# Row sums on one core: the last store as two 64-partition transfers, from SyncE and ScalarE

## The chip, the cores and the metric

The kernel runs on one core of a Trainium2 chip. The metric is the device time of one execution in microseconds (us); less is better. The engines that matter are VectorE (DVE), ScalarE (ACT) and SyncE (SP), which issues DMA transfers. A transfer works on 16 DMA engines and adds 16 in total to a semaphore as its parts land.

## The reference

The input is 67.11 MB of float32, and each row of 1,024 numbers is summed to one number:

```python
batch, seq, dim = 32, 512, 1024
x = np.random.randn(batch, seq, dim).astype(np.float32)

def reference(x):
    return np.sum(x, axis=-1).astype(np.float32)
```

## The kernel before

There are 16,384 rows, 128 for each partition. They are taken as two blocks: in the first, partition p holds 113 neighbouring rows, in the second 15 (`BLOCKS`). Rows are loaded in groups of up to 16 per partition into three buffers in turn (`xt`, `BUFS`), so that a load of group b waits until the buffer of group b - 3 has been read. DVE sums a whole group with one TENSOR_REDUCE (`rows_dve`); ACT sums some rows of the late groups one by one (`rows_act`).

Nothing is scheduled by a planner: each engine runs its instructions in the order in which `row_sums` writes them, and waits on semaphores that are set by hand. All loads are issued by SP (line 139), in the order of the list `loads`. The first two of them are moved ahead of the program's opening barrier.

The order is made so that little is left once the last bytes have come. One row per partition is loaded first (`lead`). The last 16 rows of block 0 (columns `z0` to `Z` of `res_z`) come last: three pieces cut at `CUTS`, and then the very last row in two parts (`tail`), 576 and 448 numbers wide, each summed by a DVE instruction of its own (`pairs_dve`, line 75). The second part takes the sum of the first as its first element.

The sums go out in three stores, all from SP. Two early stores (line 145) carry all columns that are done before the last 16; they are issued once `piece2` has landed. The last store (lines 146 to 148) carries the last 16 columns of block 0: 128 partitions with 64 bytes each. It waits for DVE's last count (`vec`) and for ACT's last count (`act`). Each instruction of ACT or DVE that ends a sum adds 1 to its engine's semaphore.

Behind the last store SP waits for the early stores (line 151), clears the semaphores below `store` (line 152), and then waits until `store` is 16 and takes the 16 off again (line 153). That wait is the last instruction of the program.

Of the kernel before, what the change touches and what calls it, by code (L numbers as in the profile page):

```python
# [13 lines left out]
CUT = 576  # L14
CUTS = (0, 9, 13, 15)
EARLY = 2


def row_sums(nc, x: bass.AP, out: bass.AP):
    P = nc.NUM_PARTITIONS  # L20
# [6 lines left out]
    xs, outs = [], []  # L27
# [14 lines left out]
    x_z, res_z = xs[0], sums[0]  # L42
    Z = BLOCKS[0]
    z0 = Z - G
# [3 lines left out]
    sems = {n: nc.alloc_semaphore(n) for n in names}  # L48
    slots = [sems[f"slot{i}"] for i in range(BUFS)]
    vec, act = sems["vec"], sems["act"]  # L50
# [3 lines left out]
    count = {"vec": 0, "act": 0}  # L54
# [88 lines left out]
    for k, n in enumerate(BLOCKS):  # L143
        end = z0 if k == 0 else n
        nc.sync.dma_start(out=outs[k][:, 0:end], in_=sums[k][:, 0:end]).then_inc(sems["early_store"], 16)
    nc.sync.wait_ge(vec, count["vec"])
    nc.sync.wait_ge(act, count["act"])
    nc.sync.dma_start(out=outs[0][:, z0:Z], in_=res_z[:, z0:Z]).then_inc(sems["store"], 16)


    nc.sync.wait_ge(sems["early_store"], 16 * len(BLOCKS))
    nc.sync.sem_clear(range(numbers[0], sems["store"].num))
    nc.sync.wait_ge(sems["store"], 16).then_inc(sems["store"], -16)


def kernel(tc: tile.TileContext, x: bass.AP, out: bass.AP):
    tc.close()
    tc.compile()  # L158
    nc = tc.nc
    row_sums(nc, x, out)  # L160

    sp = mybir.EngineType.SP
    fn = nc.m.functions[0]
    entry, body = None, None
    for blk in fn.blocks:
        ops = [i for i in blk.instructions if i.engine == sp]
        if entry is None:
            entry = blk  # L170
        elif any(i.opcode == "DMACopy" for i in ops):
            body = blk
            break
    code = list(body.instructions)
    loads = [i for i in code if i.engine == sp and i.opcode == "DMACopy"][:EARLY]
    for load in loads:
        assert not load.sync_info.on_wait
        code.remove(load)
    body.instructions = code
    code = list(entry.instructions)  # L180
    at = next(k for k, i in enumerate(code) if i.engine == sp and i.opcode == "Drain")
    code[at:at] = loads
    entry.instructions = code
# [29 lines left out]
```

## Time and profile before

| | us |
|---|---|
| median of 3 runs | 160.58 (160.57 to 160.62) |
| the profiled execution | 160.63 |
| its span, first to last instruction | 159.3 |
| DVE busy in the span | 121.6 (76%) |
| ACT busy in the span | 17.2 (11%) |
| HBM read | 67.11 MB, 422 GB/s over the span |
| last store, issue to landing | 1.4 (8.0 KB) |

The profile shows one execution. Its times count from the first instruction in the span. A line such as L75 is a line of the kernel; SPq stands for SP's DMA issues, whose duration is the time that SP needs to hand a transfer over and not the time in which data moves. The DMA share of a stretch is the mean busy share of the core's 16 DMA engines. Waiting is not counted as busy.

### The profile page before, as it was taken

Reading aid. Unit: us, or ns where it says so; the run is one execution under the profiler, and the core shown is the slowest. Engines: PE = TensorE matmul, PEld = TensorE weight load, DVE = VectorE, ACT = ScalarE, POOL = GpSimd, SP = SyncE. Lnnn points to the kernel's source line nnn. Section 1 sums busy time; section 2 is a strip of 40 time slices with the busy share of each in tenths; the row PEclk is TensorE's granted clock in tenths of the full one; section 3 lists DMA queues with packets and bytes.
Section 4 is the critical chain, followed back from the end, with each engine's and each line's share of the span. In section 5 each row is a group of like instructions: output and inputs, shape, how many; then the busy total and the mean of one; then the engine's idle time right before and its main releaser. Section 6 shows DMA issues by size and latency. Waiting matters only on the chain.

```text
span 159.3 us, 108 instructions
## 1 busy us (share of the span) xinstructions
DVE 121.6 (76%) x17; ACT 17.2 (11%) x31; POOL 0.2 (0%) x4
## 2 busy tenths in 40 slices
DVE  1100029999499995999869996899959999797685
ACT  3000000000000000000000000000000000394694
POOL 0000000000000000000000000000000000000000
DMA  9969979989699699699699797996996999699994
GB/s 395 527 263 527 477 313 527 411 378 527 280 510 527 263 527 527 263 527 510 280 527 444 346 527 313 477 527 263 527 510 278 463 494 494 296 444 444 395 400 143
DMA packets 2304, 67.18 MB, mean 422 GB/s; under 512 B 640, under 2 KB 768, under 8 KB 1024
## 3 DMA queue, kind: packets, MB, share of 16 engines
q1 hardware_dynamic: 2304, 67.18, 98.1%
HBM read 67.11 MB, written 0.07 MB: 422 GB/s over the span
## 4 chain that ended last, share of the span: by engine, by line
DMA 75%; DVE 22%; SPq 1%; issue 0%
DMA xt<-in_x_dram 51%; DMA tail<-in_x_dram 24%; DVE res L57 22%; SPq L139 1%; DVE pairs L75 0%; DVE res L75 0%
## 5 line engine op out<-in xcount | busy, mean ns | idle before, releaser
L57 DVE TENSOR_REDUCE res<-xt 128x16 f32<-128x16384 f32 (+3 forms) x9 | 118.7, 13191 | 32.5 <-DMA xt<-in_x_dram 32.5
L68 ACT ACTIVATE xt<-xt 128x1024 f32<-128x1024 f32 x15 | 15.6, 1043 | 138.1 <-DMA xt<-in_x_dram 138.1
L68 ACT ACTIVATION_READ_ACCUMULATOR xt<-xt 128x1 f32 x15 | 2.8, 187 | 0.0
L57 DVE TENSOR_REDUCE res<-lead 128x1 f32<-128x1024 f32 x1 | 1.2, 1220 | 1.4 <-DMA lead<-in_x_dram 1.4
L103 DVE MEMSET tail<- 128x1 f32 x1 | 0.1, 59 | 2.0 <-PEq L158 2.0
L68 ACT ACT_TABLE_LOAD x1 | 1.3, 1283 | 1.9 <-PEq L158 1.9
L75 DVE CUSTOM_DVE_ANT_0 pairs<-tail 128x288 f32<-128x288 f32 (+1 forms) x2 | 0.9, 426 | 0.1
L75 DVE CUSTOM_DVE_ANT_0 pairs<-xt 128x512 f32<-128x512 f32 x1 | 0.7, 692 | 0.2 <-DMA xt<-in_x_dram 0.2
L75 DVE DVE_READ_ACCUMULATOR2_ANT res<- 128x1 f32 x2 | 0.2, 82 | 0.0
L197 POOL MEMSET const-uint8-127<- 128x1 uint8 x1 | 0.1, 103 | 0.0
L197 POOL MEMSET const-bfloat16-1.0<- 128x1 bf16 x1 | 0.1, 102 | 0.0
L197 POOL MEMSET const-float32-0.0<- 128x1 f32 x1 | 0.1, 98 | 0.2 <-issue 0.2
L197 POOL MEMSET const-float32-1.0<- 128x1 f32 x1 | 0.1, 98 | 0.0
L75 DVE DVE_READ_ACCUMULATOR2_ANT tail<- 128x1 f32 x1 | 0.1, 80 | 0.0
## 6 DMA issues: line engine op xcount, KB each, us to landing
xt<-in_x_dram SPq DMA_DIRECT2D x1, 7680.0 KB, 39.6
xt<-in_x_dram SPq DMA_DIRECT2D x1, 4608.0 KB, 31.2
xt<-in_x_dram SPq DMA_DIRECT2D x1, 2048.0 KB, 35.7
xt<-in_x_dram SPq DMA_DIRECT2D x1, 1024.0 KB, 37.7
lead<-in_x_dram SPq DMA_DIRECT2D x1, 512.0 KB, 3.4
tail<-in_x_dram SPq DMA_DIRECT2D x1, 288.0 KB, 37.9
tail<-in_x_dram SPq DMA_DIRECT2D x1, 224.0 KB, 38.0
xt<-in_x_dram SPq DMA_DIRECT2D x6, 40.8
```

The lines of the kernel that those rows point to most:

```text
L57: nc.vector.tensor_reduce(out=res[:, c : c + n], in_=t[:, j * D : (j + n) * D].rearrange("p (j d) -> p j d", d=D), axis=X, op=ADD,).then_i ...
L68: nc.scalar.activation(out=v, in_=v, func=COPY, accum_out=res[:, c + i : c + i + 1]).then_inc(act, 1)
L75: nc.vector.tensor_tensor_reduce(out=pairs[:, 0 : h - a], in0=t[:, a:h], in1=t[:, h:b], scale=1.0, scalar=0.0, op0=ADD, op1=ADD, accum_out ...
L103: nc.vector.memset(tail[:, CUT + 15 : CUT + 16], 0.0).then_inc(vec, 1)
L139: nc.sync.dma_start(out=dst, in_=src).then_inc(s, 16)
L197: nc = _bacc.Bacc("TRN2", target_bir_lowering=False, num_devices=1)
```

## The change

The last store becomes two transfers. SP stores partitions 0 to 63, and ACT stores partitions 64 to 127; both add to `store`, which now has to reach 32. ACT waits for both counts before its transfer, and its wait for `vec` adds 1 to `act`. SP's two waits stand in the other order in the source. Ahead of clearing the semaphores SP now also waits for that extra count of `act`, so that ACT's waits are over by then.

```diff
+HALF = 64
...
+    nc.sync.wait_ge(act, count["act"])
     nc.sync.wait_ge(vec, count["vec"])
-    nc.sync.wait_ge(act, count["act"])
-    nc.sync.dma_start(out=outs[0][:, z0:Z], in_=res_z[:, z0:Z]).then_inc(sems["store"], 16)
-
-
+    nc.sync.dma_start(out=outs[0][0:HALF, z0:Z], in_=res_z[0:HALF, z0:Z]).then_inc(sems["store"], 16)
+    nc.scalar.wait_ge(act, count["act"])
+    nc.scalar.wait_ge(vec, count["vec"]).then_inc(act, 1)
+    nc.scalar.dma_start(out=outs[0][HALF:P, z0:Z], in_=res_z[HALF:P, z0:Z]).then_inc(sems["store"], 16)
+
+
+    nc.sync.wait_ge(act, count["act"] + 1)
     nc.sync.wait_ge(sems["early_store"], 16 * len(BLOCKS))
     nc.sync.sem_clear(range(numbers[0], sems["store"].num))
-    nc.sync.wait_ge(sems["store"], 16).then_inc(sems["store"], -16)
+    nc.sync.wait_ge(sems["store"], 32).then_inc(sems["store"], -32)
```

## The prediction

> **What bounds the kernel now.** I read the page first, then the chain of waits, then the waits of SyncE (SP), then the DMA activity of single stretches. The share line under the chain says that this is a load-bound kernel:
>
> ```profile
> DMA 75%; DVE 22%; SPq 1%; issue 0%
> ```
>
> The change does not touch that part. The chain in order of time (start, duration, what) shows where the loads stop deciding, and on the way it gives prices that I need for SP's DMA issues:
>
> ```profile
> 1.85 0.06 issue
> 1.92 40.18 DMA xt<-in_x_dram
> ...
> 117.56 0.33 SPq L139
> 117.89 0.04 issue
> 117.93 0.44 SPq L139
> 118.37 0.04 issue
> 118.42 0.46 SPq L139
> 118.88 0.04 issue
> 118.92 0.45 SPq L139
> ...
> 119.41 37.98 DMA tail<-in_x_dram
> 157.40 0.02 issue
> 157.42 0.40 DVE pairs L75
> 157.82 0.01 DVE res L75
> ```
>
> The last load lands at 157.40, DVE reduces it by 157.82, and all that is left is the last store. So the change can move only the 1.48 us from 157.82 to the end of the span at 159.30. SP's waits in this stretch (who waited, for whom, us in total, times, longest) are:
>
> ```profile
> SPq L153 <- SPq L153: 1.0, 1, 1.0
> SPq L148 <- DVE res L75: 0.5, 1, 0.5
> ...
> SPq L147 <- ACT xt L68: 0.3, 1, 0.3
> ```
>
> Source line 146 waits for `vec` and line 147 for `act`, but what ran is one wait instruction for `act` (L147), over early, and the wait for `vec` carried by the transfer itself (L148). So the transfer starts 0.03 us after DVE's end. The final wait (L153) then sits for 1.0 us. The rows by stretch say what happens inside that time; the last two columns are the DMA engines' busy share and GB/s:
>
> ```profile
> 157.82:158.18 0.36, 0.00 (x1) 0.00 (x0) 0.00 (x0) 1.00 0.00 0
> 158.18:158.68 0.50, 0.00 (x0) 0.00 (x0) 0.00 (x0) 1.00 0.00 0
> 158.68:158.90 0.22, 0.00 (x0) 0.00 (x0) 0.00 (x0) 1.00 0.36 38
> 158.90:159.30 0.40, 0.00 (x0) 0.00 (x0) 0.00 (x0) 1.00 0.00 0
> ```
>
> The store is 0.36 of hand-over and issue (the issue itself 0.33), 0.50 in which nothing moves, 0.22 of packets, and 0.40 until SP has seen the completion. The packets keep an engine busy for only 0.36 x 0.22 = 0.08 us. What a split halves, the rows, is at most the 0.22; the other 1.26 us is latency that each half pays again, though side by side if the two are independent.
>
> **The change part by part.** The profiled execution took 160.63 us, 1.33 more than its span; the median of the runs is 160.58. I take the 1.33 as it is, and add my differences to the median.
>
> *The order of the two waits.* Built, the changed program has on SP a wait instruction for `vec`, and then a transfer that carries the wait for `act`. The late semaphore is now on the separate instruction, so that instruction and the step to the next one lie on the path. On ScalarE (ACT) it is the same: one wait instruction for `vec` and `act` that also adds 1 to `act`, then the transfer. In the trace such a wait lasts 0.017 us, and from the end of the barrier's wait to SP's next DMA it is 0.06 (the chain's first piece). So both halves are issued at 157.82 + 0.03 + 0.02 + 0.06 = 157.93 instead of 157.85: **+0.08**. Low end +0.06, with the 0.04 that lies between SP's successive issues; high end +0.14, with the 0.12 that DVE took after the same barrier's wait.
>
> *SP's half.* Its queue has been in use all along. I take the old 0.33 + 0.50 + 0.22 + 0.40, so it ends 0.08 later than before.
>
> *ACT's half.* No row shows ACT issue a DMA. ACT's last instruction ends at 157.27, so it is idle for 0.55 us before `vec` arrives, and nothing is queued behind the transfer. The nearest row for a first use of a queue is SP's first transfer, `lead`, and its stretches:
>
> ```profile
> 0.00:0.38 0.38, 0.00 (x0) 0.00 (x0) 0.15 (x4) 1.00 0.00 0
> 0.38:1.00 0.62, 0.00 (x0) 0.00 (x0) 0.05 (x2) 1.00 0.00 0
> 1.00:1.20 0.20, 0.00 (x0) 0.00 (x0) 0.00 (x0) 1.00 1.48 246
> ```
>
> It took 0.38 to issue and another 0.62 to the first packet, against 0.33 and 0.50 for the last store: 0.05 + 0.12 = **+0.17**. That row is a load, and part of its 0.12 can belong to that; 0 is the low end. I take 0.17, since ACT's queue is as fresh as SP's was then. The high end is open; I treat more than this as a rival.
>
> *The packets.* Each half has 64 rows over the same 16 engines. If the 0.22 is proportional to the rows it becomes 0.11 (-0.11); if the engines' staggered starts make it up it stays; one completion record more on each engine adds 0.01. I take **0**: with 0.08 of work in 0.22 the stretch is mostly stagger, and that does not depend on the rows. [...]
>
> *The end.* `store` has to reach 32. The 16 increments came within 0.16 us before; the two sets could queue for up to that, but ACT's set comes 0.17 after SP's in this sum, so I take **0**.
>
> *What SP does besides.* The wait for `early_store`, the wait for ACT's extra `act` increment and the clearing come after the issue and before the final wait, some 0.1 us more than before. The 1.0 us of L153 hides them; without it they would cost that 0.1. The clearing cannot catch ACT still waiting, and ACT's increment is there by 157.9. No queue but ACT's own is passed: no load or compute changes place.
>
> Sum: 0.08 + 0.17 = **+0.25**, so 160.83 (0.16% more). Adding the ends gives -0.05 (0.06 - 0.11) to +0.48 (0.14 + 0.17 + 0.01 + 0.16), so 160.53 to 161.06 for this case alone. A difference of 0.2%, 0.32 us, is about what a measurement of this kernel can tell from no change: below 160.26 is faster, above 160.90 slower.
>
> **The rivals.**
>
> *B, slower: the two issues get in each other's way, and the change does not do what it says.* In the chain, an issue that follows at once on another takes 0.44 to 0.46 instead of 0.33, whatever its size, and the starts lie 0.37 (117.56 to 117.93), then 0.49 and 0.50 apart. Something is held for about 0.49 us by each transfer. If it belongs to SP's sequencer, ACT is free of it; if SP and ACT share it, ACT's half (or SP's) trails by 0.37 to 0.49. Then the sum is 0.08 + 0.43 = +0.51, 161.09; the ends are 0.08 + 0.37 - 0.11 = +0.34 (160.92), and 0.08 + 0.49 + 0.17 = +0.74 (161.32). It decides from a trailing of 0.24 on. Against it: this trace has one issuing engine only, so the row is equally well a matter of that engine. [...]
>
> *C, slower: ACT's first transfer costs far more than SP's first did*, in the issue or outside the span. The only thing that ACT fetches in this trace is its table, a row of 1.28 us. A start between the +0.32 that would be told and such a fetch gives 160.90 to 160.58 + 0.08 + 1.28 = 161.94. Nothing in the profile speaks for it but that ACT has never issued a DMA here; SP's cheap first use speaks against it.
>
> *D, faster: the latency shrinks with the rows.* All of SP's transfers have 128 rows, so this trace cannot say whether the 0.49 that something is held depends on the rows. If it does, 64 rows hold it for 0.24, the first packet comes 0.24 earlier and the stretch of packets loses up to 0.11: 0.08 - 0.24 = -0.16, to -0.27 (160.42 to 160.31). If the whole 0.83 before the first packet and half the 0.22 went, 0.08 - 0.42 - 0.11 = -0.45 (160.13). Against it: issues that followed at once cost 0.44 to 0.46 for 224 KB (the second of `tail`) as for 2,048 KB (117.93), so the bytes do not set the price; whether the rows do is open.
>
> **How the numbers follow.** The case summed above gets 0.40: of it 0.34 is within 0.2%, and 0.06, its upper end, beyond. B gets 0.27, all slower. C gets 0.12, all slower. D gets 0.13: 0.07 faster, 0.06 within. For what I have not thought of, 0.08: 0.02 faster, 0.03 within, 0.03 slower. Together faster 0.09, within 0.43, slower 0.48. The likeliest single case stays within 0.2%, so its 160.83 is the forecast, though most of the rest lies above it. The range 160.30 to 161.35 holds the case, all of B and the part of D that is not told from no change; outside are about 0.07 of D, 0.09 of C and 0.03 of the rest.
>
> **What would show it.** In the changed profile I look for: both transfers' issue at 0.11 after DVE's end (the order of the waits); ACT's issue at about 0.38 and SP's at 0.33 (0.44 or more on either, started together, is B); the first packets 0.50 after SP's issue and 0.62 after ACT's; the last packet to the end unchanged at 0.40. C would be a long issue or a silent stretch of over 0.8 on ACT's half, or more than 1.33 outside the span; D a first packet under 0.7 us after the issue's start. The forecast is wrong if the span's growth comes to less than 0 or more than 0.5.

## The result and the profile after

The changed kernel takes 161.26 us (median of 6 runs, 161.12 to 161.37) against 160.62 for the kernel before in the same runs: 0.64 us more, a ratio of 1.0036 with a 95% interval of 1.0026 to 1.0047. It is slower by more than 0.2%. The time lies in the predicted range; the forecast itself, 160.83, had 0.25 of the 0.64.

The chain of the changed kernel is made of the same parts as before, so the loss has to be sought behind it:

```profile
DMA 74%; DVE 22%; SPq 1%; issue 0%
```

In the timeline, the last lines are DVE's final read-out and the two issues of the split store (start, duration, engine, line):

```profile
157.81 0.08 DVE L76 DVE_READ_ACCUMULATOR2_ANT res<- 128x1 f32 x1
157.97 0.53 SPq L149 DMA_DIRECT2D out_dram<-res  x1
158.03 0.53 ACTq L152 DMA_DIRECT2D out_dram<-res  x1
```

The two transfers do start nearly together. But each issue takes 0.53 where the single one took 0.33, and both are equally long. SP's waits show that the late semaphore moved from the transfer to the wait instruction (L148, `vec`), and that the final wait (L158) grew from 1.0 to 1.3:

```profile
SPq L158 <- SPq L158: 1.3, 1, 1.3
...
SPq L148 <- DVE res L76: 0.9, 1, 0.9
```

By stretch, with the DMA engines' share and GB/s in the last two columns:

```profile
157.90:157.97 0.07, 0.00 (x0) 0.00 (x0) 0.00 (x0) 1.00 0.00 0
157.97:158.50 0.53, 0.00 (x0) 0.00 (x0) 0.00 (x0) 1.00 0.00 0
158.50:159.14 0.64, 0.00 (x0) 0.00 (x0) 0.00 (x0) 1.00 0.00 0
159.14:159.34 0.20, 0.00 (x0) 0.00 (x0) 0.00 (x0) 1.00 0.21 21
159.34:159.41 0.07, 0.00 (x0) 0.00 (x0) 0.00 (x0) 1.00 0.00 0
159.41:159.61 0.20, 0.00 (x0) 0.00 (x0) 0.00 (x0) 1.00 0.21 21
159.61:160.00 0.39, 0.00 (x0) 0.00 (x0) 0.00 (x0) 1.00 0.00 0
```

SP's half moves from 159.14 and ACT's half from 159.41. The engines rest between the two, so the halves do not overlap at all. Each half needs 0.20 for 64 rows, nearly as much as 128 rows needed (0.22), and the last stretch has not changed.

The table takes the trace's records apart from DVE's last end to the end of the span, in us. Start is the step to the issue, silent the time from the issue's end to the first packet, packets the time from the first packet's start to the last one's, rest the time from the last packet's start to the end. The experiments below are in it too. Where two halves end apart, the half that ends last is shown.

| kernel | half | start | issue | silent | packets | rest | sum |
|---|---|---|---|---|---|---|---|
| before | SP, 128 rows | 0.03 | 0.33 | 0.50 | 0.20 | 0.42 | 1.48 |
| changed | ACT, 64 | 0.14 | 0.53 | 0.85 | 0.19 | 0.40 | 2.10 |
| sp_half | SP, 64 | 0.03 | 0.53 | 0.64 | 0.19 | 0.39 | 1.77 |
| act_alone | ACT, 128 | 0.13 | 0.37 | 0.51 | 0.20 | 0.42 | 1.63 |
| split_warm | ACT, 64 | 0.14 | 0.53 | 0.85 | 0.18 | 0.42 | 2.12 |
| split_late | ACT, 64 | 1.20 | 0.52 | 0.66 | 0.18 | 0.40 | 2.96 |
| swap_only | SP, 128 | 0.08 | 0.33 | 0.50 | 0.21 | 0.42 | 1.53 |
| col_split | ACT, 128 | 0.13 | 0.37 | 0.51 | 0.19 | 0.50 | 1.70 |
| split_96_32 | ACT, 32 | 0.13 | 0.38 | 0.50 | 0.16 | 0.51 | 1.68 |
| split_96_32_carried | ACT, 32 | 0.03 | 0.40 | 0.51 | 0.16 | 0.53 | 1.63 |
| split_64_carried | ACT, 64 | 0.03 | 0.54 | 0.90 | 0.19 | 0.39 | 2.05 |

Between the first two rows lie 0.62 us: 0.11 in the start, 0.19 in the issue, 0.35 in silence, and about -0.02 each in the packets and the rest. The other 0.07 of the span's growth lies ahead of DVE's last end (157.90 against 157.82). That end differs by more among the profiled runs of this study, from 157.69 to 158.17, in kernels whose loads are the same, so I do not put it down to the change.

### The profile page after: what moved, and what is told of

The parts are those of the page before. It is cut to its first block, busy times and chain, and to the rows that moved or that the text cites. A ratio compares the mean times of both kernels' runs of the same rounds, so it can differ in the third digit from the quotient of the medians.

```text
span 160.0 us, 111 instructions
## 1 busy us (share of the span) xinstructions
DVE 121.6 (76%) x17; ACT 17.2 (11%) x31; POOL 0.2 (0%) x4
## 4 chain that ended last, share of the span: by engine, by line
DMA 74%; DVE 22%; SPq 1%; issue 0%
DMA xt<-in_x_dram 51%; DMA tail<-in_x_dram 24%; DVE res L58 22%; SPq L140 1%; DVE pairs L76 0%; DVE res L76 0%
```

## The experiments

My first reading of the two equal issues was rival B: two engines that issue at once slow each other. The first four runs set this against two others: that a transfer of 64 rows is dearer by itself, and that the first use of ACT's queue is. Kernels that ran together share their runs of the kernel before; its median was 160.88, 160.63 and 160.68 in the three groups of four. The times given are medians; the ratios are estimated from all runs of both kernels and can differ a little from the quotient of the medians.

### SP's half alone (sp_half)

```diff
-    nc.sync.dma_start(out=outs[0][:, z0:Z], in_=res_z[:, z0:Z]).then_inc(sems["store"], 16)
+    nc.sync.dma_start(out=outs[0][0:64, z0:Z], in_=res_z[0:64, z0:Z]).then_inc(sems["store"], 16)
```

> SP alone stores partitions 0 to 63 with the waits of before; ACT stores nothing, and the last 16 columns of partitions 64 to 127 are left out. In the changed kernel SP's half took 0.53 to issue and 0.65 more to its first packet, against 0.33 and 0.50 before. Contention (SP's and ACT's issues slow each other): alone, 64 rows take 0.33 and 0.50 again, 160.5 to 160.6. Shape (a transfer of 64 rows costs more to issue than one of 128): 0.53 and 0.65, some 160.96. Rows (fewer rows, shorter latency): under 0.33 and under 0.50, 160.4 or less.

Measured: 161.13 against 160.88, ratio 1.0016 (1.0007 to 1.0026). Half the work, with nothing on ACT, is slower than all of it. The issue in the timeline, and the silent stretch in the rows by stretch:

```profile
158.19 0.53 SPq L148 DMA_DIRECT2D out_dram<-res  x1
```

```profile
158.71:159.35 0.64, 0.00 (x0) 0.00 (x0) 0.00 (x0) 1.00 0.00 0
159.35:159.55 0.20, 0.00 (x0) 0.00 (x0) 0.00 (x0) 1.00 0.21 21
```

These are the changed kernel's figures for SP's half, without a second issuer. Contention does not make them, and neither does the latency fall from 128 rows to 64. What is left is the shape, which the sweeps further down take apart.

### ACT alone with the whole store (act_alone)

```diff
-    nc.sync.dma_start(out=outs[0][0:HALF, z0:Z], in_=res_z[0:HALF, z0:Z]).then_inc(sems["store"], 16)
...
-    nc.scalar.dma_start(out=outs[0][HALF:P, z0:Z], in_=res_z[HALF:P, z0:Z]).then_inc(sems["store"], 16)
+    nc.scalar.dma_start(out=outs[0][:, z0:Z], in_=res_z[:, z0:Z]).then_inc(sems["store"], 16)
...
```

> ACT alone makes the whole last store, 128 rows, as the first and only transfer of its queue; SP issues nothing then. In the changed kernel ACT's half took 0.53 to issue and 0.85 to its first packet. Contention: 0.33 to 0.38 and about 0.50, so only the later start on ACT is left, 160.7 to 160.8. A slow first use of ACT's queue: 0.53 and 0.85 stay, 161.2. Shape: as contention.

Measured: 161.05 against 160.88, ratio 1.0012 (1.0003 to 1.0022).

```profile
158.06 0.37 ACTq L151 DMA_DIRECT2D out_dram<-res  x1
```

```profile
158.43:158.94 0.51, 0.00 (x0) 0.00 (x0) 0.00 (x0) 1.00 0.00 0
158.94:159.15 0.21, 0.00 (x0) 0.00 (x0) 0.00 (x0) 1.00 0.38 39
```

ACT's first transfer costs 0.04 more to issue than SP's store and 0.01 more of silence. The 0.10 of the later start is most of its loss of 0.15 behind DVE's end. A slow first use is out.

### ACT's queue used before (split_warm)

```diff
...
+    nc.scalar.dma_start(out=warm[:, :], in_=xs[0][:, 0:16]).then_inc(sems["warm"], 16)
...
```

> The changed kernel with one small load (8 KB into a scratch tile that nothing reads) issued by ACT at the start, so that the store is not the first transfer of ACT's queue. Contention: the store's issues stay at 0.53 and ACT's half at 0.85 to the first packet, 161.2 to 161.3. Slow first use: ACT's half falls to SP's figures or to 0.33 and 0.50, 160.8 to 161.0.

Measured: 161.48 against 160.88, ratio 1.0036 (1.0023 to 1.0049), as the changed kernel; ACT's half at 0.53 and 0.85 as before. The use of the queue lay some 156 us ahead of the store, so a queue that cools within that time is not excluded by this run alone; act_alone, never used before and cheap, excludes it.

### ACT's half later (split_late)

```diff
-    nc.scalar.wait_ge(act, count["act"])
-    nc.scalar.wait_ge(vec, count["vec"]).then_inc(act, 1)
+    nc.scalar.wait_ge(vec, count["vec"])
+    nc.scalar.activation(out=lead[:, :], in_=lead[:, :], func=COPY).then_inc(act, 1)
+    nc.scalar.wait_ge(act, count["act"] + 1).then_inc(act, 1)
...
-    nc.sync.wait_ge(act, count["act"] + 1)
+    nc.sync.wait_ge(act, count["act"] + 2)
```

> The changed kernel with one ACTIVATE of 128x1024 (about 1.05 us, its result is not used) between ACT's wait and its transfer, so that SP's half has its first packets before ACT issues. Contention: both halves go back to 0.33 of issue and about 0.50 to the first packet; the end comes about 1.1 us later than with one store, 161.8 to 161.9. Shape: 0.53 and 0.65 for SP's half all the same, and the end at 162.2 or more. Slow first use: SP's half at 0.33 and 0.50, ACT's half at 0.53 and 0.85, 162.3.

Measured: 162.30 against 160.88, ratio 1.0089 (1.0074 to 1.0104). ACT's issue and its silence, when SP has long been done:

```profile
159.37 0.52 ACTq L153 DMA_DIRECT2D out_dram<-res  x1
```

```profile
159.89:160.54 0.65, 0.00 (x0) 0.00 (x0) 0.00 (x0) 1.00 0.00 0
```

The issue stays long without company. The silence falls from 0.85 to 0.66 by the records (the stretch above has 0.65, its ends being rounded). So there is contention too, in the silence of the half that comes second: 0.19 us. SP's half kept 0.52 and 0.64.

### Which shapes are dear (shapes)

```diff
+    nc.sync.wait_ge(sems["store"], 16)
+    nc.sync.dma_start(out=outs[0][0:128, z0:Z], in_=res_z[0:128, z0:Z]).then_inc(sems["probe"], 16)
+    nc.sync.wait_ge(sems["probe"], 16)
+    nc.sync.dma_start(out=outs[0][0:64, z0:Z], in_=res_z[0:64, z0:Z]).then_inc(sems["probe"], 16)
+    nc.sync.wait_ge(sems["probe"], 32)
...
```

> The kernel of before, and behind its last store thirteen small transfers by SP, each waiting for the one ahead to land, so that each is alone: stores of 128, 64 (0 to 63), 64 (64 to 127), 32, 96, 112, 120 and 16 partitions with 16 columns, 128 partitions with 8 columns, 64 with 32, loads of 128 and 64 partitions with 16 columns, and the first again. SP's half alone took 0.525 to issue and 0.64 to its first packet. Full width is the cheap case: 0.33 and 0.50 wherever all 128 partitions take part, 0.52 or more and over 0.6 in all others, also for 112. Count by engine (it follows the rows): a graded price, dearest at 16 rows and near 0.33 at 112. Bytes (4 KB is dearer than 8 KB): 64 partitions with 32 columns are as cheap as 128 with 16, and 128 with 8 as dear as 64 with 16. Place in the output alone: the loads do not differ.

In the timeline the stores of L153 to L165 have 128, 64, 64, 32, 96, 112 and 120 partitions, the two loads of L173 and L175 have 128 and 64:

```profile
159.43 0.33 SPq L153 DMA_DIRECT2D out_dram<-res  x1
160.87 0.54 SPq L155 DMA_DIRECT2D out_dram<-res  x1
162.62 0.47 SPq L157 DMA_DIRECT2D out_dram<-res  x1
164.30 0.35 SPq L159 DMA_DIRECT2D out_dram<-res  x1
165.68 0.33 SPq L161 DMA_DIRECT2D out_dram<-res  x1
167.09 0.32 SPq L163 DMA_DIRECT2D out_dram<-res  x1
168.49 0.38 SPq L165 DMA_DIRECT2D out_dram<-res  x1
...
174.33 0.36 SPq L173 DMA_DIRECT2D lead<-in_x_dram  x1
175.97 0.52 SPq L175 DMA_DIRECT2D lead<-in_x_dram  x1
```

Each line is one transfer of one execution. None of my four guesses holds. The dear ones are the four transfers of 64 partitions, stores and load, and only they. Their silence is 0.65 to 0.66 for stores (0.76 for the load, against 0.61 for the load of 128); the stores of all other counts have 0.43 to 0.50. Here are the silent stretches of the first 64 and of the 96:

```profile
161.41:162.05 0.64, 0.00 (x0) 0.00 (x0) 0.00 (x0) 1.00 0.00 0
166.00:166.50 0.50, 0.00 (x0) 0.00 (x0) 0.00 (x0) 1.00 0.00 0
```

The bytes do not matter here (64 partitions with 32 columns are as dear, 0.47 to issue, 128 with 8 as cheap, 0.36). Alone and from start to start, 64 partitions took 1.75 and 1.68 us, 128 took 1.44, 32 took 1.38 and 16 took 1.31.

### The same split by columns (col_split)

```diff
-    nc.sync.dma_start(out=outs[0][0:HALF, z0:Z], in_=res_z[0:HALF, z0:Z]).then_inc(sems["store"], 16)
+    nc.sync.dma_start(out=outs[0][:, z0:z0 + 8], in_=res_z[:, z0:z0 + 8]).then_inc(sems["store"], 16)
...
-    nc.scalar.dma_start(out=outs[0][HALF:P, z0:Z], in_=res_z[HALF:P, z0:Z]).then_inc(sems["store"], 16)
+    nc.scalar.dma_start(out=outs[0][:, z0 + 8:Z], in_=res_z[:, z0 + 8:Z]).then_inc(sems["store"], 16)
```

> The changed kernel with the halves cut by columns: SP stores the first 8 of the 16 last columns of all 128 partitions, ACT the other 8. Waits and engines as in the changed kernel. If the price is that of a transfer of 64 partitions: both issues at 0.33 to 0.37, SP's first packet 0.50 later, and the time between before and the changed kernel, +0.15 to +0.35 over before (the upper end if ACT's half still trails by the 0.19 of the two meeting). If the price is that of 4 KB transfers or of two engines issuing at once: 0.53 each and +0.6.

Measured: 160.86 against 160.63, ratio 1.0013 (1.0004 to 1.0022). Two engines issue at the same time as in the changed kernel, and the issues are short:

```profile
157.99 0.33 SPq L149 DMA_DIRECT2D out_dram<-res  x1
158.05 0.37 ACTq L152 DMA_DIRECT2D out_dram<-res  x1
```

ACT's silence is 0.51, the same as alone: with this shape the second half does not trail. What is left is the later start (0.10), ACT's longer issue (0.04) and a rest of 0.50 instead of 0.42.

### The order of the waits alone (swap_only)

```diff
-    nc.sync.wait_ge(vec, count["vec"])
-    nc.sync.wait_ge(act, count["act"])
+    nc.sync.wait_ge(act, count["act"])
+    nc.sync.wait_ge(vec, count["vec"])
```

> The kernel of before with SP's last two waits in the order of the changed kernel, and one transfer of 128 partitions as before. The wait for vec becomes an instruction of its own: SP's transfer starts 0.07 after DVE's end instead of 0.03, +0.05. If the order of the waits were a main part of the loss, +0.3 or more.

SP's waits show `vec` on its own instruction (L147), as in the changed kernel:

```profile
SPq L147 <- DVE res L75: 0.9, 1, 0.9
```

In the trace the step is 0.075 instead of 0.028, +0.05 as expected. The times, 160.76 against 160.63, ratio 1.0008 (0.9999 to 1.0017), do not tell it from nothing.

### Both halves on SP (sp_both)

```diff
-    nc.sync.dma_start(out=outs[0][:, z0:Z], in_=res_z[:, z0:Z]).then_inc(sems["store"], 16)
+    for h in (slice(0, 64), slice(64, P)):
+        nc.sync.dma_start(out=outs[0][h, z0:Z], in_=res_z[h, z0:Z]).then_inc(sems["store"], 16)
...
```

> SP issues both 64-partition halves itself, one behind the other, with the waits of before. The first half is as SP's half alone (0.53 and 0.64). If each 64-partition issue holds SP for 0.53 and the second pays some 0.1 more, as 128-partition issues do that follow at once, the second half's first packet comes 0.6 to 0.7 after the first half's, and the time is 0.9 to 1.0 over before: worse than the changed kernel, whose second engine then saves about 0.3. If two engines in turn cost as much as one, it equals the changed kernel, +0.6.

Measured: 161.54 against 160.63, ratio 1.0056 (1.0043 to 1.0070), +0.91. The timeline has both issues in one line, 1.16 us from the first's start to the second's end (0.53 and 0.59):

```profile
157.87 1.16 SPq L149 DMA_DIRECT2D out_dram<-res  x2
```

So the second engine does save about 0.3 against issuing both halves from one, but a store that is not cut has no second half to save.

### 96 and 32 partitions (split_96_32)

```diff
-HALF = 64
+HALF = 96
```

> The changed kernel with HALF = 96: SP stores 96 partitions, ACT 32, nothing else changed. Alone, stores of 96 and of 32 partitions took 0.33 and 0.35 to issue and 0.50 to the first packet, 64 partitions 0.47 to 0.54 and 0.65. If 64 is a dear number by itself: both issues near 0.35 and 0.50, the rest after DVE's end 1.6 to 1.7 (2.10 in the changed kernel, 1.48 before), +0.1 to +0.2 over before. If two engines that issue at once are what is dear, or any part of 128: 0.5 and more again, +0.6.

Measured: 160.77 against 160.68, ratio 1.0010 (1.0000 to 1.0020). One number changed, and most of the loss is gone:

```profile
157.78 0.35 SPq L149 DMA_DIRECT2D out_dram<-res  x1
157.84 0.38 ACTq L152 DMA_DIRECT2D out_dram<-res  x1
```

### The same with the late wait carried (split_96_32_carried)

```diff
-    nc.sync.wait_ge(act, count["act"])
     nc.sync.wait_ge(vec, count["vec"])
+    nc.sync.wait_ge(act, count["act"])
...
-    nc.scalar.wait_ge(act, count["act"])
-    nc.scalar.wait_ge(vec, count["vec"]).then_inc(act, 1)
+    nc.scalar.wait_ge(vec, count["vec"])
+    nc.scalar.wait_ge(act, count["act"])
     nc.scalar.dma_start(out=outs[0][HALF:P, z0:Z], in_=res_z[HALF:P, z0:Z]).then_inc(sems["store"], 16)
+    nc.scalar.wait_ge(act, count["act"]).then_inc(act, 1)
```

> As the split of 96 and 32 partitions, with the late wait for vec carried by each transfer, as on SP before; ACT adds its 1 to act behind its transfer. The step from DVE's end to the issue falls from 0.07 (SP) and 0.13 (ACT) to about 0.03: 0.1 less than the split of 96 and 32, level with before or up to +0.1. Nothing in the parts gives time back below before: the shortest of them, 32 partitions, was only 0.06 shorter alone than 128, and ACT's issue is 0.04 longer than SP's.

Measured: 160.77 against 160.68, ratio 1.0005 (0.9996 to 1.0014): not told from before. The issues start together, 0.03 behind DVE's end:

```profile
157.72 0.34 SPq L149 DMA_DIRECT2D out_dram<-res  x1
157.72 0.40 ACTq L152 DMA_DIRECT2D out_dram<-res  x1
```

The sum behind DVE's end is still 1.63 against 1.48: ACT's issue has 0.07 more, the rest 0.11 more, the packets 0.05 less. Of the 0.1 that I expected against the split of 96 and 32, the parts show 0.05 (1.68 to 1.63), and the times show nothing. This is the best split that I found, and it does not beat one transfer.

### The changed kernel with the late wait carried (split_64_carried)

The edit is that of the last kernel, with `HALF = 64` as it was.

> The changed kernel with the late wait for vec carried by each transfer, ACT's 1 to act behind its transfer, and the halves of 64 partitions as they are. It takes away the term of the waits alone: ACT's issue 0.10 earlier, 0.1 less than the changed kernel, +0.5 over before. If the waits were the cause, it would be level with before.

Measured: 161.23 against 160.68, ratio 1.0030 (1.0019 to 1.0042). The two issues now start within 0.01 of each other:

```profile
157.77 0.53 SPq L149 DMA_DIRECT2D out_dram<-res  x1
157.78 0.54 ACTq L152 DMA_DIRECT2D out_dram<-res  x1
```

ACT's start falls by 0.10, but issue and silence of its half are 0.06 longer, so the sum falls by 0.05 only. The packets' records say why. ACT's first packet comes 0.27 after SP's first packet here, as in the changed kernel and in split_warm, although the issues start 0.005 apart here and 0.06 apart there. So in these three kernels the second half's first packet is tied to the first half's, and the time follows SP's half, which starts 0.05 earlier here than in the changed kernel.

### More shapes (shapes2)

> As the first sweep, with stores by SP of 48, 80, 60, 40, 56, 72, 88, 104, 24 and 8 partitions, 64 from partition 32 on, 64 with 4 columns, and 128. If the dear thing is four rows for an engine: 60, 40 and 56 (15, 10 and 14 engines with four rows each) are dear too, if these are divided so. If it is the number 64: only the two of 64 partitions take 0.47 or more and 0.65, wherever they start and however narrow they are. If it is a place: 64 from partition 32 on is cheap.

The edit is that of the first sweep with other counts. L153 to L171 are 48, 80, 60, 40, 56, 72, 88, 104, 24 and 8 partitions, L173 is 64 from partition 32 on, L175 is 64 with 4 columns; of the ten counts, four are shown:

```profile
159.49 0.34 SPq L153 DMA_DIRECT2D out_dram<-res  x1
...
162.24 0.38 SPq L157 DMA_DIRECT2D out_dram<-res  x1
163.57 0.28 SPq L159 DMA_DIRECT2D out_dram<-res  x1
164.79 0.32 SPq L161 DMA_DIRECT2D out_dram<-res  x1
...
172.48 0.62 SPq L173 DMA_DIRECT2D out_dram<-res  x1
174.29 0.49 SPq L175 DMA_DIRECT2D out_dram<-res  x1
```

Again only the two transfers of 64 partitions are dear: 0.62 and 0.49, with a silence of 0.64 and 0.66. Every other count took 0.28 to 0.38 and 0.43 to 0.50.

The two sweeps show one thing more. From start to start, a lone store goes with the number of its completion records (records of 4 bytes; the last store of before left 16 of them beside its 128 of 64 bytes) more than with its rows: 16, 32 and 48 partitions left 16 records and took 1.31 to 1.38 us, while 24 partitions left 12 and took 1.25, 40 left 10 and took 1.23, 8 left 8 and took 1.16. A split into two such counts, 88 and 40 for instance (1.30 and 1.23 alone), was not tried. By these figures I estimate it at about level with one transfer: ACT's part would be 0.15 shorter than the 32 partitions of the best split, which was 0.15 behind.

## Why the prediction was right or wrong

*What bounds the kernel* held: the loss lies behind DVE's last end but for 0.07 that varies from run to run.

*The order of the waits* held: +0.08 predicted for both engines, 0.05 on SP (swap_only) and 0.11 on ACT measured. Taken away in the changed kernel, it gives only 0.05 back (split_64_carried): that is SP's part of it, and ACT's half is tied to SP's.

*SP's half* is the step that failed. "I take the old 0.33 + 0.50 + 0.22 + 0.40" put no price on a shape that the trace of before did not show. sp_half measures it: 0.53 and 0.64, 0.34 more up to the first packet. I had bounded the rows only in the packets and, in D, with a sign of the other kind. The trace had transfers of 128 rows alone, and I wrote that in D; the same open question belonged into the sum, with a bound above as well as below.

*ACT's half* was wrong in size and in cause. +0.17 was taken for the first use; act_alone shows 0.05 at most for that, and split_warm no gain from an earlier use. The row it came from, `lead` with 0.38 and 0.62, shows a load rather than a first use: the load of 128 partitions in shapes, though of 8 KB only, took 0.36 and 0.61 on a queue long in use. The 0.19 + 0.35 that ACT's half lost in issue and silence are 0.31 of shape (split_late's 0.52 and 0.66 less act_alone's 0.37 and 0.51), 0.04 of ACT as the issuer (act_alone) and 0.19 of the two halves meeting (split_late).

The whole 0.62 can also be followed along SP's half: 0.05 for its later start, 0.34 for the shape, 0.27 from its first packet to ACT's, and 0.04 less in packets and rest. This way of counting gives the 0.05 that split_64_carried gained; the sum of ACT's own parts would have given 0.10. So what ACT adds by itself, in its start and its issue, lies inside the 0.27.

*The packets* held: 0.20 for 64 rows, 0.22 for 128 by the rows by stretch. None of the splits beat the single transfer. In the changed kernel the halves come one after the other (from 159.14 and from 159.41, for 0.20 each), and 0.19 of the loss goes with that, but 0.34 go with the shape (sp_half), and col_split and split_96_32 overlap and are still not faster (ratios 1.0013 and 1.0010).

*The end* held in the changed kernel (0.40), whose halves end apart; where they end nearly together the rest grew by 0.08 to 0.11 (col_split, split_96_32, split_96_32_carried), within the 0.16 that I had as its bound. *What SP does besides* held too: the clearing was over at 158.65, 1.34 ahead of the end of the span, inside the last wait.

*Rival B* came nearest in time, 161.09, and not for its reason. The issues hardly lengthen each other: 0.53 together, 0.53 and 0.52 apart, and 0.02 more on ACT where both start within 0.01 (the two carried kernels). What is left of B is the 0.19 of silence, with 64-partition transfers alone. No run shows that SP and ACT share what I had each transfer hold for 0.49, an estimate from SP's issues alone: ACT's issue of 128 partitions beside SP's took 0.372 (col_split) against 0.369 alone (act_alone). The wait that the halves of 64 do show, the 0.19, lies behind the issue.

*Rival C* is refuted by act_alone (0.04 more to issue and 0.01 more of silence). *Rival D* has the right direction for counts other than 64, but the first packet comes far less early than the 0.24 that I put for half the rows: 0.03 to 0.05 earlier for 56, 60 and 72 partitions. From start to start these took 1.31 to 1.32 against 1.44 for 128. (D's lowest sum speaks of the whole 0.83 and takes off half of it, 0.42.)

The signs that I had named did not tell the cases apart. Both issues over 0.44 and started together was to be B, a silence of over 0.8 on ACT's half was to be C; both came (0.53, and 0.85), and neither rival was the main cause. The last sign, a growth of the span by more than 0.5, did say that the forecast was wrong: the span grew by 0.69, of which 0.62 lie behind DVE's last end.

The chances named slower as the likeliest of the three outcomes, at 0.48, while the forecast took the likeliest single case within 0.2%. That the time lies in the range is luck as far as the mechanism goes: the summed case ended at 161.06, and the range reached to 161.35 only to take in B, whose reason the runs do not bear out.

## What to carry to other kernels

Before a transfer is cut, measure one transfer of the new shape alone: of two transfers side by side each paid the whole latency here (ACT's half in col_split 0.37 to issue and 0.51 of silence, as the whole store alone on ACT), and a store that is mostly latency (here 0.08 us of packets in 1.48 us) has little to halve. If an earlier trace holds one shape only, put a bound on both sides of a new shape's issue and first packet. And keep the late semaphore on the transfer itself: an instruction of its own for it costs 0.05 on SP and 0.10 on ACT in the traces, too little for the times of these runs to tell.

## What the runs showed of the hardware that was not expected

A transfer of exactly 64 partitions was dear in these runs. It took 0.47 to 0.62 to issue and 0.64 to 0.66 of silence as a lone store, against 0.28 to 0.38 and 0.43 to 0.51 for lone stores of 8, 16, 24, 32, 40, 48, 56, 60, 72, 80, 88, 96, 104, 112, 120 and 128 partitions. It was so on SP and on ACT (0.53 and 0.64 in sp_half, 0.52 and 0.66 for ACT's half in split_late), as a store and as a load (one load: 0.52 and 0.76, against 0.36 and 0.61 for 128 partitions), from partition 0, 32 and 64 on (0.54, 0.62 and 0.47 to issue), and at 16, 64 and 128 bytes a row (0.49, 0.47 to 0.62 and 0.47).

If a completion record is taken for an engine, it is not a matter of four rows for each engine: a half of 64 left 16 of these records in the changed kernel, and stores of 60, 40 and 56 partitions left 15, 10 and 14 in shapes2. So these have four rows for each record too, and took 0.38, 0.28 and 0.32 to issue. By the same count the 16 engines hold for the transfers of the kernel before, all of 128 rows, and not for every count of rows. Why 64 is dear stays open, and so does why the second of two such transfers sends its first packet 0.27 after the first one's, 0.19 later than by itself, while two of 128 partitions, or of 96 and 32, followed each other within 0.07 to 0.11.
